# Layer-norm affine moved from GpSimd into two fused VectorE operations, and the gating unit spread over slots 9 to 12

## The chip, the cores and the metric

One core of a Trainium2 chip runs the whole program. The metric is the device time of one execution in microseconds; the kernel before has a median of 1228.44 us over three runs (1226.77 to 1230.06).

The engines go by the names of the profile: PE is TensorE's matmul and PEld its weight load, DVE is VectorE, ACT is ScalarE, POOL is GpSimd, SP is SyncE, which here issues nearly all loads. Each engine works through its own list of instructions in order, and the lists meet at semaphores.

## The reference, cut to what matters

Two layers, each FFN, mixer, FFN. The mixer projects the normed input to queries, keys, values, two gating inputs `u` and `v`, and two branch gates. The part that the change touches is the spatial gating unit:

```
def layer_norm(x, g, b):
    mu = mean(x);  xc = x - mu
    y = xc * rsqrt(mean(xc * xc) + LN_EPS)
    return y * g + b

def spatial_gating(u, v, ln_g, ln_b, w_s, b_s):
    vn = layer_norm(v, ln_g, ln_b)              # (256, 1024), by row
    s = einsum('gts,bnsgc->bntgc', tril(w_s), vn) + b_s
    return u * s
```

`u` and `v` come through a GELU. The result goes through a branch projection, next to the attention branch, and both are merged and projected out. Everything is float32, and a matmul operand is split into a high and a low part (three products for one).

## The kernel before, in words

Tokens are two row tiles of 128 (t = 0 and 1). Weights arrive as units of 128x1024 float32, 512 KB each, in a fixed order over the whole program (class `Stream`). A unit is loaded by SP (L113) into one of four raw buffers, then split: ACT writes the high part (L131), DVE the low part (L132). When a unit has been split, its raw buffer is free and the load of the unit four further on is issued; nine split units can be held.

The schedule is written out by hand (`manual_schedule`): the order of the Python calls is the order of each engine's list. `project` at the end of a sub-layer already starts the first part of the next one (`FirstMix`: `v`, keys and values of the mixer). Per row tile, `finish` evacuates these from PSUM, and the `turn` function that it returns transposes the keys and does the layer norm of `v`: statistics, a reciprocal square root in small DVE operations, then the normalising. For t = 0 the turn is called late in `project`, for t = 1 in slot 4 of `middle`.

`middle` goes through 48 slots, one weight unit each: slots 0 to 7 make `u`, 8 to 15 the queries, then the branch gate b, the gating branch's projection, gate a, and the attention branch's projection. A slot is 24 matmuls (L239 to L241), followed by the split of the unit of seven slots later; every second slot a finished pair is evacuated one slot late (queries: ACT L784, DVE L786, both halves of the split). So "the unit of slot 15" is split in slot 8, and its load waits for the split of the unit of slot 11. The call `at((slot, 0), fn)` puts other work in front of a slot's matmuls, `at((slot, 1), fn)` behind them. Slot 4 carries the turn of t = 1, slot 5 carries `early`, which has SP load the two gain rows of the next norms (L205) into the two buffers that hold the layer norm's gain and bias, and slot 14 carries the first attention call (scores at L675, L676: 16 matmuls over four pairs of heads, in order; the last eight need the queries of slots 10 and 11, whose evacuation stands behind slot 12's matmuls).

`gating(g)` handles two of the eight groups: 8 matmul instructions of PE (L651) on the normed `v` and the masked weights, then DVE adds the bias (L654) and multiplies by `u` (L657), ACT writes the high part (L149) and DVE the low part (L150). `GATING` lists the slots for groups 0, 2, 4 and 6: before, groups 0 and 4 both stand in front of slot 8.

Of the kernel before, what the change touches and what calls it, by code (L numbers as in the profile page):

```python
# [17 lines left out]
ALU = mybir.AluOpType  # L18
# [34 lines left out]
WARM = (11, 8)  # L53

ATTEND = (14, 17, 20, 24, 27, 29)
GATING = (8, 10, 8, 11)


@with_exitstack
def trunk(ctx: ExitStack, tc: tile.TileContext, a: dict, out: bass.AP):  # L60
    nc = tc.nc
# [23 lines left out]
    def new(p, shape, tag, dt=F32, **kw):  # L85
        ids[0] += 1
        return p.tile(shape, dt, tag=tag, name=f"{tag}_{ids[0]}", **kw)

    def f(ap):
        return ap.bitcast(F32)  # L90
# [61 lines left out]
    def halves():  # L152
        return [slice(h * 512, (h + 1) * 512) for h in range(2)]
# [5 lines left out]
    def rsqrt(sums):  # L159


        ys, ws = [], []
        for v, k in sums:
            y = new(tiny, [P, 1], "ry")
            nc.vector.tensor_scalar(out=y.bitcast(I32), in0=v.bitcast(I32), scalar1=-0.5,
                                    scalar2=float(0x5F3759DF + (k << 23)), op0=ALU.mult, op1=ALU.add)
            ys.append(y)
        for v, k in sums:
            w = new(tiny, [P, 1], "rw")
            nc.vector.tensor_scalar(out=w, in0=v, scalar1=-0.5 / 4.0 ** k, scalar2=None, op0=ALU.mult)  # L170
            ws.append(w)
        for _ in range(3):
            ts = []
            for y, w in zip(ys, ws):
                t = new(tiny, [P, 1], "rt")
                nc.vector.scalar_tensor_tensor(out=t, in0=y, scalar=w, in1=y, op0=ALU.mult, op1=ALU.mult)
                ts.append(t)
            for i, t in enumerate(ts):
                y = new(tiny, [P, 1], "ry")
                nc.vector.scalar_tensor_tensor(out=y, in0=t, scalar=1.5, in1=ys[i], op0=ALU.add, op1=ALU.mult)  # L180
                ys[i] = y
        return ys
# [8 lines left out]
    def bank():  # L191
        return new(mm, [P, 512], "mm")
# [7 lines left out]
    def rows_of(t):  # L200
        return slice(t * P, (t + 1) * P)
# [54 lines left out]
    class FirstFFN:  # L256
# [25 lines left out]
        def finish(self, t, r, hts):  # L282

            o = self.o[t]
            s = new(t2, [P, 512], "t2")
            hh = new(t2, [P, 512], "t2")
            if r is None:
                nc.scalar.activation(s, o[0], AF.Silu)
                nc.vector.tensor_tensor(out=hh, in0=s, in1=o[1], op=ALU.mult)
            else:  # L290
                nc.scalar.activation(s, o[0], AF.Silu, scale=r)
                nc.vector.scalar_tensor_tensor(out=hh, in0=o[1], scalar=r, in1=s, op0=ALU.mult, op1=ALU.mult)

            def turn():
                split(hts[0][0][:, 0:FA, rows_of(t)], hts[0][1][:, 0:FA, rows_of(t)], transpose4(hh, 0))
            return turn

    class FirstMix:
# [37 lines left out]
        def finish(self, t, r, kv):  # L336
            vs, vv, kth, ktl, lng, lnb = kv
            sc = 1.0 if r is None else r
            o2 = self.kv[t]

            kd = new(t2, [P, NKV, 2, HD], "t2")
            ksrc = o2[:, P:2 * P].rearrange("p (g d) -> p g d", g=NKV)
            for i in range(2):
                nc.vector.tensor_scalar(out=kd[:, :, i, :], in0=ksrc, scalar1=sc, scalar2=None, op0=ALU.mult)
            for o, b in zip(self.o[t], halves()):
                nc.scalar.activation(vs[:, t, b], o, AF.Gelu, scale=sc)

            vsrc = o2[:, 0:P].rearrange("p (g d) -> p g d", g=NKV)
            nc.scalar.activation(vv[:, t, :, 0, :], vsrc, AF.Copy, scale=sc)
            nc.vector.scalar_tensor_tensor(out=vv[:, t, :, 1, :], in0=vsrc, scalar=sc,  # L350
                                           in1=f(vv[:, t, :, 0, :]), op0=ALU.mult, op1=ALU.subtract)

            def turn():
                kp = bank()[:, 0:NKV * P].rearrange("p (a b) -> p a b", a=NKV)
                for g in range(NKV):
                    nc.tensor.transpose(kp[:, g, :], kd[:, g, :, :].rearrange("p r d -> p (r d)"), ident)
                nc.scalar.copy(kth[:, :, rows_of(t)], kp)
                for r in range(2):
                    b = slice(r * HD, (r + 1) * HD)
                    nc.vector.tensor_tensor(out=ktl[r][b, :, rows_of(t)], in0=kp[b], in1=f(kth[b, :, rows_of(t)]),  # L360
                                            op=ALU.subtract)

                sums = new(tiny2, [P, 2, 6], "st")
                for h in range(2):
                    nc.vector.bn_stats(sums[:, h, :], vs[:, t, h * 512:(h + 1) * 512])
                mv = new(tiny2, [P, 2], "mv")
                nc.vector.bn_aggr(mv, sums.rearrange("p a b -> p (a b)"))
                ve = new(tiny, [P, 1], "rv")
                nc.vector.tensor_scalar(out=ve, in0=mv[:, 1:2], scalar1=LN_EPS, scalar2=None, op0=ALU.add)
                rs, = rsqrt([(ve, 0)])  # L370
                nc.vector.tensor_scalar(out=vs[:, t, :], in0=vs[:, t, :], scalar1=mv[:, 0:1], scalar2=rs,
                                        op0=ALU.subtract, op1=ALU.mult)
                nc.gpsimd.tensor_tensor(out=vs[:, t, :], in0=vs[:, t, :], in1=lng, op=ALU.mult)
                nc.gpsimd.tensor_tensor(out=vs[:, t, :], in0=vs[:, t, :], in1=lnb, op=ALU.add)
            return turn


# [232 lines left out]
    class Mix:  # L610
# [128 lines left out]
        def middle(self, xt, xth, xtl, turn1, early):  # L739
# [3 lines left out]
            def at(slot, fn):  # L743
                todo.setdefault(slot, []).append(fn)
# [25 lines left out]
            self.ysh, self.ysl = new(m8, [P, G, S], "m8", F32R), new(m8, [P, G, S], "m8", F32R)  # L770
            for i, slot in enumerate(GATING):
                at((slot, 0), lambda i=i: self.gating(2 * i))
# [270 lines left out]
```

## Time and profile before

| | us |
|---|---|
| median of three runs | 1228.44 |
| the profiled execution | 1228.25 |
| its span in the trace | 1226.5 |
| PE busy in the span | 1184.1 (97%) |
| DVE busy | 844.3 (69%) |
| ACT busy | 674.9 (55%) |
| POOL busy | 82.1 (7%) |

The span runs from the first to the last instruction; 1.75 us of the execution lie around it. Shares of busy time are means over stages with different limits, so the rows below are taken from the stage around the change: 225 to 280 us in the first layer. The mixer of the second layer repeats the same pattern some 604.3 us later.

### The profile page before, as it was taken

Reading aid. Unit: us, or ns where it says so; the run is one execution under the profiler, and the core shown is the slowest. Engines: PE = TensorE matmul, PEld = TensorE weight load, DVE = VectorE, ACT = ScalarE, POOL = GpSimd, SP = SyncE. Lnnn points to the kernel's source line nnn. Section 1 sums busy time; section 2 is a strip of 40 time slices with the busy share of each in tenths; the row PEclk is TensorE's granted clock in tenths of the full one; section 3 lists DMA queues with packets and bytes.
Section 4 is the critical chain, followed back from the end, with each engine's and each line's share of the span. In section 5 each row is a group of like instructions: output and inputs, shape, how many; then the busy total and the mean of one; then the engine's idle time right before and its main releaser. Section 6 shows DMA issues by size and latency. Waiting matters only on the chain.

```text
span 1226.5 us, 18552 instructions
## 1 busy us (share of the span) xinstructions
PE 1184.1 (97%) x7031; PEld 1053.6 (86%) x7031; DVE 844.3 (69%) x1431; ACT 674.9 (55%) x1155; POOL 82.1 (7%) x48
## 2 busy tenths in 40 slices
PE   8999999989999799999999999998999997999997
PEld 7888888989999688888888888888999995888886
DVE  6778657787665767675577766588865758667743
ACT  5666545446665456565455665454566654656541
POOL 0000000221112000000000000004011130000000
PEclk9999999999999899999999999999999998999999
DMA  7676764545345636557636657734643454465560
GB/s 240 192 271 214 241 203 151 175 169 175 105 134 162 216 103 224 193 186 242 221 101 223 213 200 233 230 129 166 197 141 110 150 158 157 155 209 186 193 202 34
DMA packets 61289, 220.90 MB, mean 180 GB/s; under 512 B 7056, under 2 KB 7056, under 8 KB 61200
## 3 DMA queue, kind: packets, MB, share of 16 engines
q1 hardware_dynamic: 60912, 219.46, 54.9%
q8 instruction: 55, 0.90, 0.3%
q14 instruction: 34, 0.28, 0.1%
q10 hardware_dynamic: 288, 0.27, 0.1%
HBM read 218.65 MB, written 1.05 MB: 179 GB/s over the span
## 4 chain that ended last, share of the span: by engine, by line
PE 78%; DVE 9%; ACT 5%; issue 3%; DMA 3%; POOL 2%; SPq 0%; DVEq 0%; ACTq 0%; POOLq 0%
PE mm L252 32%; PE mm L232 28%; PE mm L239 4%; PE mm L240 4%; PE mm L241 4%; DVE wl L132 3%; ACT wh L131 2%; DMA raw<-in_ffn_w 2%; PE mm L197 1%; PE mm L651 1%; ACT t L694 1%; DMA raw<-in_w_in 1%; POOL t L829 1%; DVE t L682 1%; DVE m L132 1%
## 5 line engine op out<-in xcount | busy, mean ns | idle before, releaser
L132 DVE TENSOR_TENSOR wl<-raw,wh 128x1024 fp32r<-128x1024 f32 x372 | 459.1, 1263 | 157.4 <-ACT wh L131 152.0
L131 ACT CAST wh<-raw 128x1024 fp32r<-128x1024 f32 x372 | 377.9, 1049 | 122.3 <-PE mm L232 59.1
L252 PE MATMUL mm<-xt,wh 128*128 128x512 f32 x1152 | 290.7, 393 | 0.8 <-DVE xt L885 0.7
L232 PE MATMUL mm<-wh,m 128*128 128x512 f32 x832 | 259.5, 391 | 0.0
L252 PEld LDWEIGHTS mm<-xt,wh 128*128 128x128 f32 x1152 | 207.3, 189 | 38.7 <-DVE xt L885 1.2
L232 PEld LDWEIGHTS mm<-wh,m 128*128 128x128 f32 x832 | 156.8, 188 | 32.2
L252 PEld LDWEIGHTS mm<-xt,wl 128*128 128x128 f32 x1152 | 157.1, 190 | 11.3
L232 PE MATMUL mm<-wl,m 128*128 128x512 f32 x416 | 162.3, 390 | 0.0
L252 PE MATMUL mm<-xt,wl 128*128 128x256 f32 x1152 | 160.6, 282 | 0.0
L239 PE MATMUL mm<-xt,wh 128*128 128x256 f32 x512 | 147.6, 288 | 0.0
L240 PE MATMUL mm<-xt,wh 128*128 128x256 f32 x512 | 146.3, 286 | 0.0
L241 PE MATMUL mm<-xt,wl 128*128 128x256 f32 x512 | 146.2, 286 | 0.0
L600 DVE TENSOR_TENSOR t<-mm,t 128x256 f32<-128x256 f32 x144 | 60.7, 421 | 93.7 <-ACT t L599 93.7
L239 PEld LDWEIGHTS mm<-xt,wh 128*128 128x128 f32 x512 | 99.9, 195 | 0.3
L240 PEld LDWEIGHTS mm<-xt,wh 128*128 128x128 f32 x512 | 99.8, 195 | 0.3
L241 PEld LDWEIGHTS mm<-xt,wl 128*128 128x128 f32 x512 | 99.7, 195 | 0.0
L149 ACT CAST m<-t 128x256 fp32r<-128x256 f32 (+1 forms) x104 | 45.5, 438 | 87.6 <-DVE t L657 34.5
L232 PEld LDWEIGHTS mm<-wl,m 128*128 128x128 f32 x416 | 78.4, 188 | 16.0
L602 ACT ACTIVATE t<-t 128x256 f32<-128x256 f32 x72 | 30.1, 418 | 95.4 <-DVE t L600 95.4
L599 ACT COPY t<-mm 128x256 f32<-128x256 f32 x144 | 53.1, 369 | 46.3 <-PE mm L252 46.2
L239 PE MATMUL mm<-m,wh 128*128 128x256 f32 x256 | 72.9, 285 | 0.0
L241 PE MATMUL mm<-m,wl 128*128 128x256 f32 x256 | 72.4, 283 | 0.0
(149 smaller groups left out, 1378.5 us busy)
## 6 DMA issues: line engine op xcount, KB each, us to landing
raw<-in_ffn_w SPq DMA_DIRECT2D x264, 512.0 KB, 4.5
raw<-in_w_in SPq DMA_DIRECT2D x84, 512.0 KB, 4.4
raw<-in_w_sgu_branch SPq DMA_DIRECT2D x16, 512.0 KB, 4.3
raw<-in_w_attn_branch SPq DMA_DIRECT2D x16, 512.0 KB, 4.1
raw<-in_w_out SPq DMA_DIRECT2D x16, 512.0 KB, 3.7
gain<-in_ffn_post_g SPq DMA_DIRECT2D x4, 512.0 KB, 6.6
gain<-in_ffn_pre_g SPq DMA_DIRECT2D x3, 512.0 KB, 5.0
x<-in_x SPq DMA_DIRECT2D x4, 256.0 KB, 4.3
```

Source lines behind the costliest of these rows:

```text
L131: nc.scalar.copy(h, raw)
L132: nc.vector.tensor_tensor(out=lo, in0=raw, in1=f(h), op=ALU.subtract)
L149: nc.scalar.copy(h, src)
L197: nc.tensor.transpose(ps[:, k, :], src[:, (c0 + k) * P:(c0 + k + 1) * P], ident)
L232: nc.tensor.matmul(o, every[i][0], every[i][1], start=start and i == 0, stop=stop and i == 2)
L239: nc.tensor.matmul(o, wh[:, ks], ah[:, k, :], start=(k == 0), stop=False)
L240: nc.tensor.matmul(o, wh[:, ks], al[:, k, :], start=False, stop=False)
L241: nc.tensor.matmul(o, wl[:, ks], ah[:, k, :], start=False, stop=(k == KD - 1))
L252: nc.tensor.matmul(out_, w[:, k * P:(k + 1) * P], x, start=(i == 0), stop=(i == len(todo) - 1))
L599: nc.scalar.copy(y[:, half, :], o[half][:, S:2 * S])
L600: nc.vector.tensor_tensor(out=y[:, half, :], in0=o[half][:, 0:S], in1=y[:, half, :], op=ALU.add)
L602: nc.scalar.activation(y[:, 0, :], y[:, 0, :], AF.Silu)
```

## The change

The normalising operation (subtract mean, multiply by the reciprocal root) and POOL's two operations (multiply by gain, add bias) become two `scalar_tensor_tensor` operations of DVE: (v - mean) * gain, then times the root plus bias. The four gating calls move to slots 9, 10, 11 and 12.

```
-GATING = (8, 10, 8, 11)
+GATING = (9, 10, 11, 12)
...
-                nc.vector.tensor_scalar(out=vs[:, t, :], in0=vs[:, t, :], scalar1=mv[:, 0:1], scalar2=rs,
-                                        op0=ALU.subtract, op1=ALU.mult)
-                nc.gpsimd.tensor_tensor(out=vs[:, t, :], in0=vs[:, t, :], in1=lng, op=ALU.mult)
-                nc.gpsimd.tensor_tensor(out=vs[:, t, :], in0=vs[:, t, :], in1=lnb, op=ALU.add)
+                nc.vector.scalar_tensor_tensor(out=vs[:, t, :], in0=vs[:, t, :], scalar=mv[:, 0:1], in1=lng,
+                                               op0=ALU.subtract, op1=ALU.mult)
+                nc.vector.scalar_tensor_tensor(out=vs[:, t, :], in0=vs[:, t, :], scalar=rs, in1=lnb,
+                                               op0=ALU.mult, op1=ALU.add)
```

## Rows read from the trace of the kernel before

**Rows 1.** The page: span, then busy time, share and instructions by engine.

```profile
span 1226.5 us, 18552 instructions
...
PE 1184.1 (97%) x7031; PEld 1053.6 (86%) x7031; DVE 844.3 (69%) x1431; ACT 674.9 (55%) x1155; POOL 82.1 (7%) x48
```

**Rows 2.** Waits of PE: who waited for whom, total us, times, longest us.

```profile
PE mm L197 <- DVE t L418: 16.4, 3, 8.3
PE mm L651 <- POOL n L374: 8.5, 2, 4.3
```

**Rows 3.** Timeline of PE in slot 8: start, length, instruction, idle time before.

```profile
248.99 0.39 PE L651 MATMUL mm<-wt,n 128*128 128x128 f32 x2
253.63 3.32 PE L651 MATMUL mm<-wt,n 128*128 128x128 f32 x14 [4.26 <-POOL n L374]
```

**Rows 4.** Timeline of DVE around the norm and the gating.

```profile
229.92 0.81 DVE L371 TENSOR_SCALAR n<-n,mv,ry 128x1024 f32<-128x1024 f32 x1
230.65 1.22 DVE L132 TENSOR_TENSOR wl<-raw,wh 128x1024 fp32r<-128x1024 f32 x1
...
233.73 8.24 DVE L132 TENSOR_TENSOR wl<-raw,wh 128x1024 fp32r<-128x1024 f32 x5 [0.65 <-ACT wh L131]
241.90 0.85 DVE L360 TENSOR_TENSOR ktl<-mm,kth 64x256 fp32r<-64x256 f32 x2
...
246.13 0.81 DVE L371 TENSOR_SCALAR n<-n,mv,ry 128x1024 f32<-128x1024 f32 x1
246.86 8.94 DVE L132 TENSOR_TENSOR wl<-raw,wh 128x1024 fp32r<-128x1024 f32 x4
255.83 0.69 DVE L654 TENSOR_TENSOR t<-mm,sb 128x512 f32<-128x512 f32 x1
...
262.07 2.36 DVE L132 TENSOR_TENSOR wl<-raw,wh 128x1024 fp32r<-128x1024 f32 x2 [0.74 <-ACT wh L131]
264.34 0.68 DVE L654 TENSOR_TENSOR t<-mm,sb 128x512 f32<-128x512 f32 x1
...
270.23 0.69 DVE L654 TENSOR_TENSOR t<-mm,sb 128x512 f32<-128x512 f32 x1
...
274.54 1.41 DVE L786 SCALAR_TENSOR_TENSOR m<-mm,m 64x512 fp32r<-64x512 f32 x2
```

**Rows 5.** Timeline of PE at slot 14: last projection matmul, first and ninth score matmul.

```profile
275.84 0.28 PE L241 MATMUL mm<-xt,wl 128*128 128x256 f32 x1
275.96 0.22 PE L675 MATMUL mm<-kth,m 128*128 128x128 f32 x1
...
276.81 0.27 PE L675 MATMUL mm<-kth,m 128*128 128x128 f32 x1
```

**Rows 6.** DVE groups, L132 in 238.6 to 246, L413 whole span: busy us, mean ns.

```profile
L132 DVE TENSOR_TENSOR wl<-raw,wh 128x1024 fp32r<-128x1024 f32 x3 | 3.5, 1211 | 0.0
...
L413 DVE SCALAR_TENSOR_TENSOR x<-t,ry,x 128x512 f32<-128x512 f32 x24 | 17.8, 750 | 0.6
```

**Rows 7.** Timeline of ACT behind the first turn.

```profile
232.48 0.28 ACT L349 ACTIVATE vv<-mm 128x128 fp32r<-128x128 f32 x1 [4.95 <-DVE t L344]
...
238.90 1.05 ACT L131 CAST wh<-raw 128x1024 fp32r<-128x1024 f32 x1 [1.88 <-DMA raw<-in_w_in]
```

**Rows 8.** Loads issued in 207.5:209, 250:257, 476:482: KB, median us to landing.

```profile
raw<-in_w_in SPq DMA_DIRECT2D x1, 512.0 KB, 3.8
...
raw<-in_w_in SPq DMA_DIRECT2D x3, 512.0 KB, 7.1
...
raw<-in_ffn_w SPq DMA_DIRECT2D x3, 512.0 KB, 6.3
```

**Rows 9.** Stretches: length, PE, PEld, DVE, ACT, POOL busy, PEclk granted, DMA, GB/s.

```profile
253.50:257.00 3.50, 3.37 (x16) 3.37 (x17) 3.43 (x4) 0.00 (x0) 0.08 (x1) 0.53 0.49 170
...
425.60:429.00 3.40, 3.39 (x11) 2.79 (x12) 3.28 (x7) 1.27 (x3) 0.00 (x0) 0.50 0.04 17
429.00:433.00 4.00, 4.00 (x16) 3.31 (x15) 3.75 (x12) 2.54 (x7) 0.00 (x0) 0.72 0.00 0
```

## The prediction

> **What bounds the kernel now.** I read the page first: PE is busy for 1184.1 of 1226.5 us [rows 1], so the time is PE's own work plus the places where PE stands still. The waits of PE come next, because they name those places: two of 4.3 us at the gating matmuls for POOL's second operation, one in each layer, 8.5 us together [rows 2]. The timeline of PE shows what one costs. PE starts the gating in front of slot 8 at 248.99, stands for 4.26 us, and then needs 3.32 us for 14 matmuls [rows 3]. At the pace of nine score matmuls, (276.81 - 275.96) / 8 = 0.106 us each [rows 5], they would need 1.5, so 1.8 us more are lost; the granted clock of that stretch is 0.53 [rows 9], near the lower of the two levels, 1.2 of 2.4 GHz. With 4.26 that makes 6.1 us in a layer, 12.2 in both.
>
> Then I read the timeline of DVE, because the change gives DVE work, and it decides the case. From the end of the first turn to slot 14 DVE is nearly without a gap [rows 4]. The evacuation of the second pair of queries (L786) starts at 274.54 and lasts 1.41, so it ends at 275.95. The first use of it is the ninth score matmul at 276.81 [rows 4, 5]. PE is thus only 0.86 us behind DVE at slot 14, although it has just stood still for 4.3 us at slot 8. A PE that comes 6 us earlier finds these queries missing. So the question is not whether POOL's wait goes, but when DVE gets to 274.54.
>
> **The change part by part, first layer.** The sum is made against the profiled execution's own 1228.25 us; the median, 1228.44, lies 0.2 above it.
>
> PE. Without gating, slot 8's matmuls start at 248.99. A slot is 24 matmuls at 0.12 (275.84 to 275.96) = 2.88, a gating call 8 x 0.106 = 0.85 [rows 3, 5]. Six slots and four gatings: 248.99 + 17.28 + 3.4 = 269.7 at slot 14; eight scores more, and PE reaches the ninth at 270.5.
>
> The two operations. No row has this operation at 1024 columns. L413 is the same kind at 512 and takes 0.750, 0.06 above L654's 0.69 at 512; L132 takes 1.211 at 1024 [rows 4, 6]. Lower end 1.21, upper end twice L413, 1.50; I take 1.28, L132 plus the same 0.06, as the nearest row by size. Two take 2.59 with 0.03 between them, and the next split can start 0.08 before the second ends, where it now starts 0.73 after L371 starts (229.92 to 230.65). DVE pays 2.51 - 0.73 = 1.78 us per tile.
>
> What POOL gave back. Uncontended splits follow each other by about 1.14 us ((3.5 - 1.21) / 2 [rows 6]). The five after the first turn took 8.24 in place of 4 x 1.14 + 1.21 = 5.8; the four after the second took 8.94 in place of 4.6 [rows 4]. POOL was running its two operations then, so I let 2.5 and 4.3 us come back. The Trainium skill (SBUF — State Buffer, section "SBUF: two separate sides") says that GpSimd and a VectorE operation with two SBUF inputs lock each other out for a whole instruction; the rows agree. Were the slow splits due to something that stays, 4.3 us more would stand at slot 14 in each layer, and the sum below would be 8.6 higher.
>
> First turn (t = 0). It ends 1.78 us later. ACT waits in order for what follows it (L349 [rows 7]), so the next splits begin later too, but run at full pace. If the splits alone decided, the second turn would come 0.7 us earlier (1.78 - 2.5), if nothing came back, 1.8 later. Between them stands a load: the unit of slot 10 is loaded when slot 6's is split. That now ends at 233.73 + 1.78 + 1.2 = 236.7; before, it was about 235.1, the landing at 238.90 less a load of 3.8 [rows 7, 8]. With 1.5 later ACT's cast of the unit moves from 238.90 to 240.4, and its split ends at 242.7. I take L360 at 242.64 instead of 241.90 [rows 4, 7]. The normalising then starts 4.23 later, at 246.87, and ends at 249.46. PE wants it at slot 9, at 248.99 + 2.88 = 251.9: POOL's wait is gone, with 2.4 us to spare.
>
> DVE from there, in its new order. Four splits start at 249.38 and end at 254.0. The split of slot 15's unit now stands ahead of the first gating; its load is issued when slot 11's unit is split, at 250.6. With 3.8 us [rows 8] it lands at 254.4, the cast takes 1.05, the split runs from 255.6 to 256.8: DVE idles 1.6 us. Before, the gatings stood there, and their work hid this load. The first gating takes 2.75 (half of 255.83 to 262.07 less the wait of 0.74 [rows 4]), to 259.6. The unit of slot 16 is loaded behind the two gain rows of `early`, which SP no longer holds back for POOL but issues just behind slot 15's load; at 251.7 + 7.1 [rows 8] it lands at 258.8, so its split ends about 261.1. The second gating starts at 261.05; with the first pair of queries and one split it takes 5.89 (264.34 to 270.23), to 266.94. The third, with a split, takes 4.31 less 0.1 of overlap (270.23 to 274.54), to 271.15. The fourth takes 2.75, to 273.9; ACT's half of the query evacuation is no longer hidden behind a split, 0.4, and L786 runs from 274.3 to 275.7.
>
> So the ninth score matmul starts at 275.75 instead of 276.81: 1.05 us are gained of the 6.1. POOL's wait at the gating becomes PE's wait for DVE at the scores, 270.5 to 275.75, 5.2 us.
>
> The clock. Before, PE was at full clock again long before slot 14. Now it stands still there, and restarts slow. A standstill of 4.26 us cost 1.8 above; after another of PE's long waits (three of 16.4 us together [rows 2]) a stretch of 3.4 us ran at 0.50 and one of 4.0 at 0.72, which cost 1.7 + 1.1 = 2.8 [rows 9]. Lower end 0, since no row shows a standstill of just this length; upper end 2.8. I take 2.2, between the two falls seen.
>
> Other edits cost nothing: the gating products are the same ones, moved past PE matmuls that wait for nothing; slot 14's unit is split by 254.0, 15 us before PE gets there; and SP's two gain loads wait for DVE's 249.46 instead of POOL, so SP's queue moves earlier.
>
> Sum: 1228.25 + 2 x (2.2 - 1.05) = **1230.6 us**, no change that a measurement tells (within 0.3%, or 3.7 us of the median).
>
> **The rivals.** (a) The likeliest, as worked out: 1230.6. Its own range is 1227.7 to 1233.8: 1 us either way for the walk in each layer, and the clock's cost between the two falls seen, 1.8 and 2.8.
>
> (b) The wait moves, but the clock does not fall: 1228.25 - 2.1 = 1226.2. For it: no row shows whether a fall follows here, between the scores. Against it: the gating's wait, which is shorter, had one.
>
> (c) The wait is gone for good: the full 12.2 comes back, 1216.0. For it: the page gives DVE only 69%, and POOL's wait is plain to see. DVE would have to reach the second pair of queries by 270.5, 5.2 us before my walk; without the 1.6 of idleness and with nothing paid at the first turn (1.5 at most) it is still 2 us short.
>
> (d) Slower: the load of slot 15's unit. Now DVE has nothing in front of it, so each microsecond by which it lands late is one at slot 14, in both layers. Before, that load was alone; now two gain loads are issued within 1 us of it. The row with a pair of gain loads among weight loads has 6.3 instead of 3.8 [rows 8]. With 2.5 us more: 1228.25 + 2 x (2.5 + 2.2 - 1.05) = 1235.6. It decides from 0.7 us of delay on, where the sum passes 1232.1. Against it: the 3.8 is itself that of a load with two gain loads right behind it.
>
> **How the numbers follow.** Chances: (a) 0.58, (b) 0.12, (c) 0.08, (d) 0.22. Faster by over 0.3%: all of (c), and 0.04 from the edge of (b): 0.12. Slower: 0.18 of (d) and 0.12 of (a), above 1232.1: 0.30. The same: 0.58. The range leaves out (c), 0.08, and the far end of (d), 0.08: 1223 to 1236.
>
> **What would show it.** In the changed kernel: no wait of PE at L651; DVE's splits at 1.2 us throughout; DVE waiting for ACT or a load ahead of the first L654; PE waiting for DVE in the middle of L675's 16 matmuls, about 5 us in both layers, with a granted clock near half behind it. Wrong would be: PE running through slot 14 without a wait (then c), PE waiting at L651 still, or the second L786 pair ending well before or after 275.7. If the wait is there but the clock stays at 1.00, it is (b); if the load of slot 15's unit takes over 5 us, (d).

## The result, and the profile after

The changed kernel takes 1230.93 us (median of 20 runs, 1229.15 to 1232.76), the kernel before 1227.95 (20 runs, 1225.88 to 1230.06): ratio 1.0023, 95% interval 1.0017 to 1.0029. That is 2.1 to 3.6 us slower, inside the bound of 0.3% that the prediction set for "no change", and 0.3 us above the time it named. The profiled execution took 1232.69 us, near the top of the 20, so its rows show a somewhat larger loss than the medians do.

The page of the changed kernel: span, then busy time, share and instructions by engine, against [rows 1].

```profile
span 1231.0 us, 18538 instructions
...
PE 1187.9 (96%) x7031; PEld 1057.5 (86%) x7031; DVE 838.9 (68%) x1435; ACT 675.4 (55%) x1155; POOL 55.6 (5%) x40
```

POOL loses eight operations. DVE has four more, and is yet busy for 5.4 us less than before. PE is busy for 3.8 us more with the same 7031 matmuls, which already says that some of them ran slower.

The waits of PE in the changed kernel (total us, times, longest us), against [rows 2]:

```profile
PE mm L197 <- DVE t L419: 16.5, 4, 8.3
PE mm L676 <- DVE m L787: 9.1, 2, 5.0
PE mm L676 <- DVE t L150: 2.4, 2, 1.2
```

The wait for POOL at the gating is gone in both layers. In its place stand 9.1 us at the scores (L676, formerly L675), for DVE's second pair of queries (L787, formerly L786). Lines behind the edit have moved down by one.

The timeline of PE in the changed kernel: the first matmul of slot 0, the gating, the scores of slot 14 in the first layer, and the ninth score in the second.

```profile
226.84 0.28 PE L239 MATMUL mm<-xt,wh 128*128 128x256 f32 x1
...
252.97 1.06 PE L652 MATMUL mm<-wt,n 128*128 128x128 f32 x8
...
270.92 0.22 PE L676 MATMUL mm<-kth,m 128*128 128x128 f32 x1
...
271.65 0.28 PE L677 MATMUL mm<-ktl,m 128*128 128x128 f32 x1
276.03 0.48 PE L676 MATMUL mm<-kth,m 128*128 128x128 f32 x1 [4.11 <-DVE m L787]
276.31 0.41 PE L677 MATMUL mm<-ktl,m 128*128 128x128 f32 x1
276.85 0.45 PE L676 MATMUL mm<-kth,m 128*128 128x128 f32 x1
...
278.16 0.52 PE L239 MATMUL mm<-xt,wh 128*128 128x256 f32 x1
...
881.95 0.47 PE L676 MATMUL mm<-kth,m 128*128 128x128 f32 x1 [5.04 <-DVE m L787]
```

This trace reaches slot 0 at 226.84, that of before at 225.74. The 1.10 us arise ahead of slot 0, most of them in the first 20 us of the program, and are taken off below wherever times of the two first layers are compared. The gating runs without a stop. The ninth score starts at 276.03 - 1.10 = 274.93 where it was 276.81 [rows 5], so 1.88 us are gained there, of the 6 us by which PE was ahead one slot earlier. The second layer gains 0.85 in the same way.

The stretches around these two stands, in the columns of [rows 9] (the number behind POOL is the granted clock):

```profile
269.00:272.00 3.00, 2.92 (x26) 2.78 (x24) 2.06 (x4) 1.57 (x2) 0.00 (x0) 1.00 0.48 167
...
276.00:282.00 6.00, 5.84 (x26) 5.68 (x27) 5.88 (x7) 5.74 (x7) 0.00 (x0) 0.50 0.44 137
282.00:284.00 2.00, 2.00 (x19) 2.00 (x19) 1.97 (x8) 0.00 (x0) 0.00 (x0) 0.99 0.85 258
...
882.00:889.60 7.60, 7.47 (x34) 7.31 (x35) 7.46 (x12) 5.66 (x7) 0.00 (x0) 0.50 0.53 151
889.60:892.00 2.40, 2.40 (x22) 2.40 (x22) 1.86 (x14) 0.64 (x3) 0.00 (x0) 1.00 0.90 331
```

PE restarts at half clock (1.2 of 2.4 GHz): 26 matmuls in 6 us of the first layer, 34 in 7.6 of the second, against 19 in the 2.00 us from 282 at full clock. The eight scores between 276.03 and 278.16 take 2.13 us instead of 8 x 0.11 = 0.9, a short second wait ahead of the eleventh included.

The timeline of DVE in the first layer of the changed kernel, against [rows 4], and one split of the second layer:

```profile
232.21 1.28 DVE L374 SCALAR_TENSOR_TENSOR n<-n,ry,gain 128x1024 f32<-128x1024 f32 x1
...
243.67 0.85 DVE L360 TENSOR_TENSOR ktl<-mm,kth 64x256 fp32r<-64x256 f32 x2
...
247.76 1.28 DVE L372 SCALAR_TENSOR_TENSOR n<-n,mv,gain 128x1024 f32<-128x1024 f32 x1
249.08 1.28 DVE L374 SCALAR_TENSOR_TENSOR n<-n,ry,gain 128x1024 f32<-128x1024 f32 x1
250.28 4.62 DVE L132 TENSOR_TENSOR wl<-raw,wh 128x1024 fp32r<-128x1024 f32 x4
256.31 1.22 DVE L132 TENSOR_TENSOR wl<-raw,wh 128x1024 fp32r<-128x1024 f32 x1 [1.41 <-ACT wh L131]
257.57 0.69 DVE L655 TENSOR_TENSOR t<-mm,sb 128x512 f32<-128x512 f32 x1
...
260.76 1.22 DVE L132 TENSOR_TENSOR wl<-raw,wh 128x1024 fp32r<-128x1024 f32 x1 [0.39 <-ACT wh L131]
...
275.29 1.41 DVE L787 SCALAR_TENSOR_TENSOR m<-mm,m 64x512 fp32r<-64x512 f32 x2 [0.53 <-ACT m L785]
...
866.68 1.22 DVE L132 TENSOR_TENSOR wl<-raw,wh 128x1024 fp32r<-128x1024 f32 x1 [1.31 <-ACT wh L131]
```

Four splits take 4.62 us where they took 8.94, and the pair that PE waits for still ends at 275.29 + 1.41 - 1.10 = 275.60, only 0.35 before the 275.95 of the kernel before. DVE's list from the turn to slot 14 is nearly as long as it was.

### The profile page after: what moved, and what is told of

It reads as the page before. It is cut to its first block, busy times and chain, and to the rows that moved or that the text cites. A ratio compares the mean times of both kernels' runs of the same rounds, so it can differ in the third digit from the quotient of the medians.

```text
span 1231.0 us, 18538 instructions
## 1 busy us (share of the span) xinstructions
PE 1187.9 (96%) x7031; PEld 1057.5 (86%) x7031; DVE 838.9 (68%) x1435; ACT 675.4 (55%) x1155; POOL 55.6 (5%) x40
## 3 DMA queue, kind: packets, MB, share of 16 engines
HBM read 218.65 MB, written 1.05 MB: 178 GB/s over the span
## 4 chain that ended last, share of the span: by engine, by line
PE 73%; DVE 10%; ACT 7%; DMA 5%; issue 3%; POOL 1%; SPq 0%; DVEq 0%; ACTq 0%; POOLq 0%
PE mm L252 32%; PE mm L232 28%; DVE wl L132 4%; ACT wh L131 3%; PE mm L239 3%; PE mm L240 3%; PE mm L241 3%; DMA raw<-in_ffn_w 3%; DMA raw<-in_w_in 2%; PE mm L197 1%; ACT t L695 1%; DVE t L736 1%; POOL t L830 1%; DVE t L683 1%; DVE t L150 1%
## 5 line engine op out<-in xcount | busy, mean ns | idle before, releaser
L132 DVE TENSOR_TENSOR wl<-raw,wh 128x1024 fp32r<-128x1024 f32 x372 | 446.9, 1230 | 163.5 <-ACT wh L131 158.1
L239 PE MATMUL mm<-xt,wh 128*128 128x256 f32 x512 | 149.3, 292 | 0.0
L240 PE MATMUL mm<-xt,wh 128*128 128x256 f32 x512 | 147.8, 289 | 0.0
```

The source lines that it names most:

```text
L132: nc.vector.tensor_tensor(out=lo, in0=raw, in1=f(h), op=ALU.subtract)
L239: nc.tensor.matmul(o, wh[:, ks], ah[:, k, :], start=(k == 0), stop=False)
L240: nc.tensor.matmul(o, wh[:, ks], al[:, k, :], start=False, stop=False)
```

## The experiments

The theory (T): the wait at the gating has become a wait at the ninth score, because DVE's list ends at the same point in both kernels; the little that PE gains at the ninth score (about 1 us per layer) is lost to its slow restart there. Rival R1: the wait moved, but the loss comes from elsewhere, from one half of the change. Rival R2: without the stand at slot 14, the 6 us of each layer would still not come back, because the next thing behind it is late too; against it stands R3, by which they would, and the time would go to 1216.

The table gives, for each kernel, the median, its ratio to the kernel before on the same chip, and the shift of slots against the kernel before: the start of a slot's first projection matmul less that of slot 0, minus the same in the kernel before, in us, first layer / second layer (negative is earlier; slot 14's projection stands behind the scores; "47" is the last slot of the mixer). Where a kernel moves PE's work behind a slot, it is earlier there by that work's own time: some 1.7 us of scores in e1 and e2 at slot 14, 1.9 and 0.9 of gating in e6 and e8 at slots 13 and 14. The shifts are those of one profiled run each, the ratios of all. The times in the expectations start from some 1228 us; the kernel before had medians of 1226.95 to 1227.43 beside these runs, so the ratios are what to compare.

| kernel | median, ratio [95%] | slot 13 | slot 14 | slot 16 | slot 22 | slot 30 | slot 47 |
|---|---|---|---|---|---|---|---|
| changed kernel | 1230.93, 1.0023 [1.0017, 1.0029] | -6.1 / -6.1 | -0.6 / +0.4 | +1.1 / +2.8 | +1.1 / +2.8 | +1.1 / +2.8 | +0.9 / +2.8 |
| e4, slots alone | 1231.28, 1.0036 [1.0024, 1.0047] | -4.5 / -4.4 | 0.0 / +1.0 | +2.4 / +3.4 | +2.4 / +3.4 | +2.4 / +3.4 | +2.4 / +3.4 |
| e3, operations alone | 1225.35, 0.9993 [0.9983, 1.0002] | -5.8 / -5.8 | -0.8 / -2.2 | +1.0 / -0.1 | +1.0 / -0.1 | +1.0 / -0.1 | +0.8 / -0.1 |
| e5, PE kept busy | 1224.69, 0.9977 [0.9968, 0.9986] | -6.2 / -6.1 | -1.2 / -1.1 | -1.2 / -1.1 | -1.1 / -1.0 | -0.9 / -0.8 | -0.9 / -1.0 |
| e9, before, PE kept busy | 1224.87, 0.9980 [0.9971, 0.9989] | -1.6 / -1.6 | -0.9 / -0.8 | -0.9 / -0.8 | -0.8 / -0.8 | -0.5 / -0.5 | -0.8 / -0.5 |
| e7, gain loads later | 1228.51, 1.0007 [0.9996, 1.0017] | -6.1 / -6.1 | -0.7 / -0.7 | +1.3 / +0.7 | +1.3 / +0.7 | +1.3 / +0.7 | +1.2 / +0.4 |
| e1, attention from 16 | 1224.73, 0.9981 [0.9973, 0.9990] | -6.1 / -6.1 | -7.9 / -7.8 | -6.2 / -6.0 | -7.0 / -6.8 | +0.2 / +0.6 | -0.9 / -0.9 |
| e2, attention from 15 | 1225.09, 0.9988 [0.9979, 0.9997] | -6.1 / -6.1 | -7.9 / -7.8 | -1.1 / +0.1 | -1.2 / 0.0 | 0.0 / +1.2 | -0.3 / +0.9 |
| e6, gating later | 1225.88, 0.9989 [0.9980, 0.9998] | -8.0 / -7.9 | -7.0 / -6.9 | -6.1 / -6.1 | -3.9 / -1.0 | -1.0 / +0.5 | -1.3 / +0.2 |
| e8, e6 and wider attention | 1224.38, 0.9976 [0.9967, 0.9985] | -8.0 / -7.9 | -7.0 / -6.9 | -6.1 / -6.0 | -6.2 / -6.1 | +1.5 / +1.1 | -1.8 / -1.5 |
| e10, e3 and PE kept busy | 1223.80, 0.9971 [0.9960, 0.9983] | -6.1 / -5.6 | -2.1 / -2.3 | -2.1 / -2.3 | -2.1 / -2.3 | -1.8 / -1.9 | -1.8 / -2.2 |
| e11, e7 and PE kept busy | 1223.76, 0.9971 [0.9959, 0.9982] | -6.1 / -6.1 | -1.6 / -1.2 | -1.6 / -1.2 | -1.6 / -1.2 | -1.3 / -0.9 | -1.6 / -0.9 |

Read the first row from left to right: 6 us ahead in front of the scores, nothing left behind them, and 1 to 3 us behind two slots later, when the slow stretch is over. From there to the end of the mixer nothing happens.

**Which half does it (e4 and e3).** e4 takes the kernel before and changes the slots only:

```
-GATING = (8, 10, 8, 11)
+GATING = (9, 10, 11, 12)
```

> The new gating slots alone, with GpSimd's two operations. Theory T: PE waits 1.8 us for GpSimd at slot 9 instead of 4.3 at slot 8, VectorE stays slowed by GpSimd and gets to the second query pair 0.1 to 1.6 us later than before, and PE stands there about 4.5 us with a slow restart: 1233 us (1230 to 1235), ratio 1.004. Rival: most of the wait for GpSimd goes by the slots alone, 1220 to 1224.

It came out as expected, 1.0036 for 1.004. The waits of PE in e4:

```profile
PE mm L675 <- DVE m L786: 7.9, 4, 4.0
PE mm L651 <- POOL n L374: 2.8, 2, 1.4
```

Moving the gating alone already takes POOL's wait from 8.5 to 2.8 us, and gives 7.9 to the scores. e3 is the changed kernel with the old slots, so the fused operations alone:

```
-GATING = (9, 10, 11, 12)
+GATING = (8, 10, 8, 11)
```

> The fused VectorE operations alone, with the gating calls at slots 8, 10, 8, 11 as before. Theory T: PE waits some 0.3 us at slot 8 for the norm; on VectorE two gating calls now stand where it idled for slot 15's load, so the second query pair is there 1.7 us sooner than in the changed kernel (275.0 instead of 276.7); PE stands about 2.2 us at the ninth score instead of 4 to 5: 1223.5 us (1221.5 to 1225.5, by whether the clock falls), ratio 0.996. If the new slots are a help in themselves, this is slower than the changed kernel, over 1231.

1225.35 lies at the upper end of the expected times, but by the ratio this was a miss: 0.9993, with an interval that includes 1, for 0.996. Its stands at the scores are shorter (3.57 and 2.26 us): two gating calls stand ahead of slot 15's split again, and on its timeline DVE idles there 0.74 + 1.23 us for the loads in the first layer and 0.73 in the second, against 1.41 + 0.39 and 1.55 + 1.31 in the changed kernel. Both stands are still followed by a slow stretch. So the slots cost 4.3 us alone. The fused operations alone change nothing that these runs can tell (0.9 us less by the ratio, within its noise; 0.7 more by the two mixers of the trace). Neither half removes the stand: R1 is right in that the slots are the harmful half, and what they lose is lost at slot 14, as T has it.

**The slow restart by itself (e5).** Between the eighth and the ninth score of the first attention call, 46 transposes of the identity matrix go into a PSUM region that the next scores overwrite. They compute nothing; they keep PE busy while DVE finishes.

```
+FILL = 46
...
+                for _ in range(FILL * (i == 2 and g == 0 and n == 0)):
+                    nc.tensor.transpose(s[0][:, 3, :], ident, ident)
```

> The changed kernel with 46 transposes of the identity put between the eighth and the ninth score matmul of the first attention call of each layer, in a part of the scores' bank that the later scores overwrite, so that PE works (about 4.9 us at full clock) while it would stand. Theory T: VectorE's list is the same, so the second query pair is there at the same time and the ninth score starts within 0.9 us of where it started; what goes is the slow restart. By the changed kernel's trace that is 2.5 us in the first layer and 3.1 in the second: 1225.5 us (1224 to 1227), ratio to before 0.998. Rival: the loss behind the ninth score is not the clock (the banks, the splits): 1230 to 1232.

It came out as expected. The timeline of PE in e5 at slot 14, and the stretch of 6 us behind it with its granted clock:

```profile
270.25 0.28 PE L680 MATMUL mm<-ktl,m 128*128 128x128 f32 x1
270.36 5.21 PE L674 MATMUL mm<-ident 128*128 128x128 f32 x46
275.33 0.31 PE L679 MATMUL mm<-kth,m 128*128 128x128 f32 x1
275.47 0.27 PE L680 MATMUL mm<-ktl,m 128*128 128x128 f32 x1
```

```profile
276.00:282.00 6.00, 6.00 (x52) 6.00 (x52) 5.89 (x9) 4.38 (x5) 0.00 (x0) 1.00 0.59 194
```

The fill ends when the second half of DVE's pair does (within 0.03 us in both layers). PE starts the ninth score 0.7 us later than in the first layer of the changed kernel, against slot 0, but at full clock: 52 matmuls in those 6 us where the changed kernel did 26. The time falls from ratio 1.0023 to 0.9977, which is 5.6 us (6.2 by the medians), and the shift behind the scores is -1.15 and -1.05 and stays there to slot 22. That separates the two terms of the sum. The earlier arrival at the pair is worth 1.1 us per layer. The slow restart costs 2.2 us in the first layer (+1.06 less -1.15 at slot 16). In the second the difference is 3.9, but there the pair itself is done 0.9 us later against slot 0 in the changed kernel than in e5 (50.80 and 49.92), which leaves 3.0 for the restart.

**The cushion of the kernel before (e9).** The same fill, 38 transposes, in the kernel before, in front of the gating matmuls that wait for POOL.

```
+FILL = 38
...
+                    for _ in range(FILL * (g == 0 and i == 0 and n == 1)):
+                        nc.tensor.transpose(ps[:, 1, 1, :], ident, ident)
```

> The kernel before with 38 transposes of the identity (4.1 us at full clock) put into the wait for GpSimd at the first gating call, in front of the matmuls that wait, so that PE restarts at full clock. It tells how much of the 6.1 us that stood at slot 8 could come back at all. Theory T: the slow restart there (1.8 us a layer) goes, but PE was only 0.86 us behind VectorE at the ninth score, so only 0.86 of it comes back, and PE now waits up to 0.9 us for the second query pair: 1225.3 us (1224.3 to 1226.3), ratio 0.9986. Rival, PE's own work sets the time from slot 8 on: all 3.6 us come back, 1223.4 us, ratio 0.997.

It came out as expected. In e9, PE at the gating and the one new wait:

```profile
250.20 4.31 PE L653 MATMUL mm<-ident 128*128 128x128 f32 x38
254.66 1.83 PE L654 MATMUL mm<-wt,n 128*128 128x128 f32 x14 [0.15 <-POOL n L375]
```

```profile
PE mm L678 <- DVE m L789: 0.8, 2, 0.4
```

The 14 gating matmuls take 1.83 instead of 3.32 us [rows 3]. PE is 1.6 us earlier at slots 9 to 13, and keeps 0.85 of them at slot 14, with a wait of 0.4 that is new there. The prediction had read 0.86 us between DVE and PE at that place; this is that number, measured by running into it.

**The second layer's load (e7).** In the second layer the stand was 5.04 instead of 4.11, and DVE's split of slot 16's unit waits 1.31 instead of 0.39 (866.68 and 260.76 above). e7 has the two gain rows loaded behind that unit:

```
-            at((5, 1), early)
+            at((9, 1), early)
```

> The changed kernel with the two gain loads issued in slot 9 instead of slot 5, so behind the loads of the units of slots 16 to 19. Theory T: the load of slot 16's unit lands sooner, so VectorE no longer idles for it (0.4 us in the first layer, 1.3 in the second), and the ninth score starts that much sooner: 1229 us (1228 to 1230.5), ratio to before 1.001. The wait for slot 15's unit (1.4 and 1.5 us) stays, since its load is issued ahead of the gains either way. Rival, the gain loads do nothing here: 1230.5 to 1231.5.

As expected: the two stands of e7 are 4.01 and 3.98 us, and the time is 1228.51, some 2 us less than the changed kernel by the ratios (1.0007 and 1.0023), though the two intervals touch.

```profile
PE mm L676 <- DVE m L787: 8.0, 2, 4.0
```

It is not shown that the gain loads alone delay the second layer. Of the traces with the gain loads in slot 5 and a gating call in each of slots 9 to 12, four have the second layer's pair 0.8 to 1.2 us later against slot 0 than the first layer's (the changed kernel, e1, e2, e4), but e5, with the same lists of DVE and SP, has 0.05. With the later loads it is -0.03 (e7) and 0.35 (e11). The prediction's place for a late load (slot 15's) was the wrong one: that load took 3.6 us where 3.8 was taken (DVE's idle time ahead of its split is 1.41).

**Is the lead worth anything if the stand goes (e1, e2, e6, e8).** Four kernels move work out of the way of the stand instead of filling it. e1 and e2 call the attention later:

```
-ATTEND = (14, 17, 20, 24, 27, 29)
+ATTEND = (16, 18, 21, 24, 27, 29)      # e1
+ATTEND = (15, 17, 20, 24, 27, 29)      # e2
```

> The changed kernel with the attention calls at slots 16, 18, 21, 24, 27, 29 instead of 14, 17, 20, 24, 27, 29, nothing else. Theory T: the only thing that eats the gain is PE's wait for the second query pair (4.1 and 5.0 us in the middle of the first attention call's scores) and the slow restart behind it. Two slots of 2.88 us later PE comes to the ninth score at about 277.5 of the changed kernel's trace, after the pair is there (276.7), so no wait and no fall: the 12.2 us of the wait for POOL come back, 1216 us (ratio to before 0.990). Rival R1, the extra VectorE work costs as such, wherever attention stands: 1229 to 1231. Rival R2, a later wait takes the gain (later attention calls, their transposes, the banks): 1221 to 1228.

> The changed kernel with the first attention call at slot 15 instead of 14. Theory T: a dose between: PE comes 2.88 us later, so it stands 1.3 us in the first layer and 2.2 in the second, and the restart is at full clock or nearly so: 12.2 less 4 gives 1220 us, up to 1223 if the clock falls in both layers (ratio 0.993 to 0.996). R1: 1229 to 1231.

Both were misses: e1 1224.73, not 1216, and e2 1225.09 (0.9988), not 1220 (0.993 to 0.996). In e1 there is no wait at the scores any more, and the lead of 6 to 7 us stands at slot 22; by slot 30 it is gone. The waits of PE in e1 name where:

```profile
PE mm L713 <- POOL t L703: 6.0, 4, 1.8
PE mm L713 <- DVE t L736: 3.7, 2, 1.9
PE mm L239 <- DVE t L736: 2.6, 2, 1.5
PE mm L725 <- DVE m L683: 0.9, 2, 0.4
```

These are the steps of the attention itself: POOL's division of the probabilities (L703) and DVE's work on the scores and outputs (L683, L736), 13.2 us together, 6.9 in the first layer and 6.3 in the second. In e2 one slot is not enough: it still stands at the scores (1.40 and 0.38 in the first layer, 2.65 in the second), and restarts slow.

e6 keeps the attention where it was and moves three gating calls behind the queries, so that the pair is not queued behind them:

```
-GATING = (9, 10, 11, 12)
+GATING = (9, 13, 14, 15)
```

> The changed kernel with the gating calls at slots 9, 13, 14 and 15 instead of 9, 10, 11 and 12, nothing else. VectorE's work is the same; only one gating call instead of four stands in its list ahead of the second query pair. Theory T: the pair is there 9 us sooner (267 instead of 276.7 in the changed kernel's first layer), PE does not stand at the scores, and its lead of 6 us holds up to slot 20. What run e1 showed then comes: the probabilities' transposes of slot 21, which had 3.6 us to spare in the kernel before, find GpSimd's division unfinished. So about 3 us a layer stay: 1222 us (1218 to 1225), ratio 0.995. Rival, the amount of VectorE's work and not its order decides: 1229 to 1232.

A miss again, 0.9989 for 0.995. There is no wait at the scores, a lead of 6 us holds to slot 20, and by slot 30 no more than 1 us of it is left. PE's waits in e6, and the longest of them on its timeline in the first layer:

```profile
PE mm L713 <- POOL t L703: 7.4, 4, 3.4
PE mm L713 <- DVE m L683: 3.6, 2, 2.4
```

```profile
295.47 1.09 PE L713 MATMUL mm<-ident,t 128*128 128x128 f32 x8 [1.99 <-POOL t L703]
...
322.27 1.12 PE L713 MATMUL mm<-ident,t 128*128 128x128 f32 x4 [2.40 <-DVE m L683]
```

e8 adds to e6 that a phase of the first attention calls lets four slots go by instead of three, to give POOL's division more time:

```
-            yield 3
+            yield 4 if heads[0] < 8 else 3
```

> As e6_gates_late, and the first three attention calls of each layer wait four slots instead of three between GpSimd's division and the transposes. Theory T: PE, which is ahead of VectorE by 6 us, then comes to the transposes 2.9 us later and finds them ready; more of the 12.2 us stays: 1219 us (1216 to 1223), ratio 0.993. Rival: the gain goes at the next place (the last three calls, or the merge in slots 40 to 47), and the result is that of e6.

A miss as well, 1224.38 instead of 1219 (0.9976 for 0.993). The waits for POOL are nearly gone, and the lead is still 6.9 and 6.6 us at slot 27; at slot 30 PE is 1.5 and 1.1 us behind the kernel before. The timeline of PE in e8 there:

```profile
326.45 0.38 PE L676 MATMUL mm<-kth,m 128*128 128x256 f32 x1 [0.93 <-ACT n L809]
330.40 0.58 PE L676 MATMUL mm<-kth,m 128*128 128x256 f32 x1 [3.44 <-DVE t L150]
```

Now the scores of the later attention calls wait for PSUM banks: one that ACT empties (L809, the branch gate), and one that DVE's split of the transposed probabilities (L150) frees, 3.44 us where the changed kernel waits 1.2 (its third wait above). What puts e1 and e8 ahead at the last slot they win behind slot 30: neither has the two waits of the kernel before in slot 32 (0.70 and 1.00 us) nor the stretch at half clock that follows them there (0.50 from 349.3 to 352.7). So R2 holds and R3 falls: three schedules without the stand at slot 14 end 1.1 to 3.3 us ahead of the kernel before over their two mixers, not 12. The lead is taken back between slots 21 and 30 each time, by another step of the attention. Which step would be last with all of them rearranged is not settled by these runs. A fifth raw buffer, which might shorten DVE's idle time for the loads, was not tried.

**The best of the parts (e10 and e11).** e10 has the fused operations, the old slots and a fill of 28; e11 the changed kernel with e7's later loads and a fill of 40.

```
-GATING = (9, 10, 11, 12)                # e10
+GATING = (8, 10, 8, 11)
+FILL = 28
...
-            at((5, 1), early)           # e11
+            at((9, 1), early)
+FILL = 40
```

> The fused operations with the gating calls at their old slots (as e3_affine_only) and 28 transposes of the identity between the eighth and the ninth score of the first attention call. Theory T: the second query pair stays 2.5 to 3 us sooner than in the changed kernel, as in e3, and the slow restart goes, as in e5: 1225.4 less 2.5 a layer, 1220.5 us (1219 to 1222.5), ratio 0.995. Rival, PE's lead is taken back in slots 21 to 29 as in e6 and e8: 1223 to 1225.

> The changed kernel with the gain loads in slot 9 (as e7) and 40 transposes between the eighth and the ninth score (as e5). Theory T: both act apart: e5's 1224.7 less the 0.4 and 1.3 us by which the second pair comes sooner, 1223 us (1222 to 1224.3), ratio 0.9965. Rival, the gain loads did nothing and e7 was lucky in its clock: 1224.7.

e11 came out as expected, e10 was a miss, 3 us above its expectation (1223.80 for 1220.5): in its trace it gains 2.1 and 2.3 us at slot 14 and keeps nearly all of it, 4.0 in both mixers, and the median shows 3.6. So it was not the lead that was taken back, as its rival had it. The expectation had started from e3's median, 1225.4, which looks better than e3's trace (0.7 behind the kernel before over the two mixers). Against that trace e10 is 3.0 and 2.2 us earlier at slot 16, near the 2.5 that was expected. Both beat the kernel before by 0.17% to 0.41%, and the changed kernel by more. None of these runs found more at this place with the attention as it is.

## Why the prediction was right

- **POOL's wait goes.** Right. The normed `v` is ready at 249.08 + 1.28 - 1.10 = 249.26 (249.46 predicted), PE's gating comes at 251.87 (251.9).
- **The price of the two operations.** Right: 1.28 us each, the value that came from the half-size row plus 0.06 [rows 6].
- **What POOL gives back to DVE.** Right. The groups of L132 in the stage from slot 0 to slot 14 say it in one line each, before (225 to 280) and after (225 to 281):

```profile
L132 DVE TENSOR_TENSOR wl<-raw,wh 128x1024 fp32r<-128x1024 f32 x17 | 26.8, 1618 | 1.7 <-ACT wh L131 1.6
```

```profile
L132 DVE TENSOR_TENSOR wl<-raw,wh 128x1024 fp32r<-128x1024 f32 x17 | 20.2, 1221 | 4.2 <-ACT wh L131 4.1
```

  The same 17 splits take 6.6 us less (2.5 + 4.3 = 6.8 predicted). In both layers that is 13.2; the four L372 and four L374 add 4 x 2.56 = 10.2 and the four L371 of [rows 4] go with 4 x 0.81 = 3.2, so DVE should be busy for 6.2 us less; the page says 5.4. It was POOL's operations and not the new slots: e4, which has both, still takes 26.9 us for these 17 splits. Behind the second turn of the kernel before, POOL's two operations and the two splits that start inside them stand like this:

```profile
247.08 3.22 POOL L373 TENSOR_TENSOR n<-n,gain 128x1024 f32<-128x1024 f32 x1 [9.60 <-ACT wh L131]
250.38 3.20 POOL L374 TENSOR_TENSOR n<-n,gain 128x1024 f32<-128x1024 f32 x1
...
247.99 3.39 DVE L132 TENSOR_TENSOR wl<-raw,wh 128x1024 fp32r<-128x1024 f32 x1
...
251.31 3.35 DVE L132 TENSOR_TENSOR wl<-raw,wh 128x1024 fp32r<-128x1024 f32 x1
```

  Each of the two splits ends 1.1 us behind the end of the POOL operation in which it started. The rule of the Trainium skill that the prediction weighed (SBUF — State Buffer, section "SBUF: two separate sides": the two engines lock each other out) is borne out by these rows.
- **DVE's walk to the second pair.** Right to 0.2 us at its points: ACT's cast of slot 10's unit, which waits for its load, at 240.35 (240.4), L360 at 242.57 (242.64), idle for slot 15's load 1.41 (1.6), slot 16's split done at 260.88 (261.1), the pair done at 275.60 (275.7). One slip of 0.1 is in it: 236.7 less 235.1 is 1.6, where the prediction goes on with 1.5. So the saved 6.6 us of a layer can be followed: 2.5 are idle time of DVE in front of splits (1.7 before, 4.2 after, behind the second bar of the two rows above), 2 x 1.78 = 3.6 pay the two operations in both turns, and 0.35 is left at the pair.
- **PE's stand.** Right in place and cause, a little off in length: 4.1 and 5.0 us for 5.2. The prediction had the ninth score wait for the whole pair. L787 is two instructions; the ninth score starts at 276.03, while the pair ends at 276.70, and only the eleventh, at 276.85, comes behind that. So 1.88 and 0.85 us were gained at the ninth, not 1.05; e5, in which the ninth score starts when the second half is done, has the 1.15 and 1.05 of the walk.
- **The slow restart.** Right that it follows, and about right in size in the first layer: 2.2 us per layer were taken, with 2.8 as the upper end. From the ninth score to slot 16 the shift goes from -1.88 to +1.06 in the first layer and from -0.85 to +2.81 in the second, 2.9 and 3.7 us. But 0.7 of that in the first is the wait for the second half of the pair, which e5 has too. By e5 the restart itself costs 2.2 in the first layer and 3.0 in the second, by the comparison above. The falls the price was taken from were shorter [rows 9]; here PE runs at 0.50 for 6.0 and 7.6 us after it restarts.

Together the trace has -1.88 - 0.85 + 2.9 + 3.7 = +3.9 for the two places (+3.8 at the ends of the two mixers) where the prediction had 2 x 1.15 = +2.3; the medians have +3.0. What the prediction missed is nearly all in the second layer (the first has +1.06 for +1.15): the pair came 0.9 us later there than in the first, and its slow stretch was longer. That the time named is hit to 0.3 us is in part luck: it starts from a run of 1228.25, where the median is 1227.95, and its change is 0.6 us too small. Of the rivals, (b) falls with the clock rows, (c) with the wait, and (d) with slot 15's load, though the second layer has a mild form of it one load later (1.31 us of DVE's idle time ahead of slot 16's split).

A general rule stood against the prediction. The Trainium skill (Perfetto Trace Analysis, section "Optimization Strategies") advises, when the matmul engine waits for other engines, to optimize those that block the critical path. Here the blocking engine was relieved entirely, and the time did not fall: the 8.5 us of waiting for it became 9.1 us of waiting for the next one.

## What to carry to other kernels

Before pricing a wait as its length, read where the bound engine next meets another list, and how much sooner that list gets there: here 0.86 us, of 6 that were to be gained, and in these runs the rest could not be had. A stand of the bound engine that only moves is not free: here it was followed by a slow restart at its new place too, which cost more than the earlier arrival had gained. Two cheap probes help with such questions: fill the stand with work that computes nothing (what comes back is about the restart's price), and move the next meeting away (what comes back is what the lead is worth as far as the meeting after it).

## What the runs showed of the hardware

After stands of 4.1 and 5.0 us PE ran at half clock for 6.0 and 7.6 us of work, longer than the stretch that followed the 4.3 us stand of the kernel before, 3.50 us at a granted clock of 0.53 [rows 9]. The length of a stand alone did not tell what followed. In the first layer of e2, stands of 1.40 and 0.38 us were followed by 7.1 us at 0.52 (273.3 to 280.4); in the first layer of e6, a stand of 1.99 us was followed by 6.6 us at 1.00 (295.4 to 302).

Transposes of a 128x128 identity, one each 0.11 us, were enough to hold the granted clock at 1.00 through the same place (e5, e9). The changed kernel with that fill was 5.6 us of 1231 faster (e5), some 5 of them the restart's. In e9 it was 2.6 us by the medians (0.0020 of the kernel before), of which the trace shows 0.8 and 0.5 in the mixers; where the rest comes from is not shown.

And an engine that took work over was busy for less time: POOL's operations in the same stage had stretched DVE's two-input splits from 1.22 to a mean of 1.62 us.
